# Two latent product pairs in one pass, and the next stage's gate rows and lambda made during the input projections

## The chip, the cores and the metric

One Trainium2 chip, one of its cores. The time is device microseconds of one launch. The kernel before took 2594.69 us (median of 3 runs, 2593.53 to 2594.82). The profiled execution took 2595.66 us, its span 2593.9 us, at a mean granted TensorE clock of 0.975 of full speed.

## The reference

One layer of an encoder with two attention branches over 2048 prompt tokens and 8 x 16 sample tokens that continue streams of 2048 cached positions. All of it is fp32.

```
h   = rms_norm(x, g_in)
qa, ka, va, z_a, qd, ckv_in, kpe_in, z_b, m_a, m_b = split(h @ w_in)
q1, q2, k1, k2 = rope of qa and ka, 4 heads            # differential branch
lam = exp(sum(lq1*lk1)) - exp(sum(lq2*lk2)) + lam_init
attn_a = (softmax(q1 k1) - lam * softmax(q2 k2)) v
q   = rms_norm(qd, g_qa) @ w_uq ; ckv = rms_norm(ckv_in, g_kva)   # latent branch, 4 heads
attn_b = softmax(q_nope . (ckv w_uk) + q_pe . kpe) (ckv w_uv)
y   = sigmoid(m_a) * (attn_a*silu(z_a)) @ w_oa + sigmoid(m_b) * (attn_b*silu(z_b)) @ w_ob
x   = rms_norm(x + y @ w_out)
```

Both softmaxes are causal by chunks of 64 tokens. New keys, values and latent rows are outputs too.

## The kernel before

Every fp32 product is made of three passes on TensorE: both factors are split into a high and a low part (`_split`, `_mm3`, L100 to L102 and L114/L115), and hi x hi, lo x hi, hi x lo are added in PSUM. For activations the split is a multiplication with the norm's factor on VectorE (scalar_tensor_tensor), a cast on ScalarE, and a subtraction on VectorE.

The program has these stages.

- *Input projections* (`_phase_a`). Three parts of the tokens (2 x 384, 2 x 384, 2 x 320). A part begins with its token rows x (L201 DMA, L202 scaling, L204 cast, L205 subtraction) and the product psv for the values (L246 to L248), which reads the first of them. Then come 11 pairs of column blocks. Each pair is made of seven products p1 to p7 in place of eight (`pair_products`, L327): p1 to p4 read the token tiles X[0], X[1]; p6, p7, p5 read sums of them, S[1], S[2], S[0]. Additions on VectorE (L335) put the seven together. The first pair is a latent one, eight rope and gate pairs follow, and the last two of a part are latent pairs again (l10 and l12 by name). Seven PSUM banks are shared by the products.
- *Latent stage* (`_phase_a2`). Six groups of 384 tokens (the last has 256): latent query products qn and qp, keys kn, values vb.
- *Attention* (`_phase_b`). Four heads of eight blocks; a block of the differential branch (sd, ed, od) runs paired with one of the latent branch (sm, em), so that each of the 32 pairs holds about the same work. At its start stands `_lam` (L1022), two small matmuls lam_ps and an exponential that give lam.
- *Sample tokens* and *output projections* at the end.

The gate columns (z_a, z_b, m_a, m_b) that the pairs don't make are made by `_gates` (L423): for each token group g, 16 units z_0 to z_15 of 24 matmuls each, all into one PSUM bank (tile z, freed by the tanh zt, L464). A unit loads 512 KB of weights (zs, two staging tiles) and splits them to zw (four tiles, two units' worth). Group 1 also writes its split weights to memory (wz, 1 MB a unit), and groups 2 and 5 read them back. A group's own rows are split first, into z_hi and z_lo (L433 to L443): one tile each, in the places that X[0] has in the input projections.

The order of instructions on each engine is set by a list scheduler that goes by priorities in program order. `_gates` is called after attention, so its matmuls come last by priority and fill places where TensorE would stand. Its loads, splits and tanh are raised (`ahead()`) to just behind the input projections.

```
_phase_a(c)
prio = tc.cur_priority
_phase_a2(c)
_phase_b(c)
for g in (0, 1, 2, 5):
    _gates(c, prio, g, None, g in (2, 5))
```

Of the kernel before, what the change touches and what calls it, by code (L numbers as in the profile page):

```python
# [46 lines left out]
def _consts(c, pool):  # L47
    nc = c.nc
    c.ident = pool.tile([P, P], F32, name="ident")
    make_identity(nc, c.ident)  # L50
    c.ones = pool.tile([P, P], F32, name="ones")
    nc.gpsimd.memset(c.ones, 1.0)
    c.mhalf = pool.tile([P, 64], F32, name="mhalf")
    nc.gpsimd.memset(c.mhalf, -0.5)
    c.vec = pool.tile([P, 20], F32, name="vec")
    nc.sync.dma_start(c.vec, c.i["vec"])
    c.g_in = c.vec[:, 0:8]
    c.g_qa = c.vec[:, 8:12]
# [70 lines left out]
def _phase_a(c):  # L129

    nc, tc = c.nc, c.tc
    with (
# [194 lines left out]
        def pair_products(p, u, nm):  # L327
# [13 lines left out]
            p4 = product(f"p4{nm}", a22, X[0], two)  # L341
            p6 = product(f"p6{nm}", s2, S[1], one)
            add(v, p6, m1)
            add(m1, p2, m1)
            p7 = product(f"p7{nm}", s3, S[2], one)
            add(u3, p7, v)
            p5 = product(f"p5{nm}", s1, S[0], one)
            add(v, p5, v)
            add(w, p5, u3)
            add(v, p3, v)  # L350
            add(u3, p4, u3)
            return (m1, v), (u3, w)

        def rope_pair(p, u, dst, pair, out, scale):
            t0, n = PARTS[p]
            res = pair_products(p, u, f"r{u}_{p}")
            for half in range(2):
# [21 lines left out]

        def latent_pair(p, u, out):  # L380
            t0, n = PARTS[p]
            res = pair_products(p, u, f"l{u}_{p}")
            for i, z in enumerate(res):
                for half in range(2):
                    nc.sync.dma_start(out[i][:, t0 + half * n : t0 + half * n + n], z[half])

        def gate_pair(p, u, out):
            t0, n = PARTS[p]
            res = pair_products(p, u, f"g{u}_{p}")
            for i in range(2):  # L390
# [5 lines left out]
        def pairs(p):  # L396
            rope = [lambda a=a: rope_pair(p, 2 * a, c.Qs, a, None, DIFF_SCALE) for a in range(2)]
            rope += [lambda a=a: rope_pair(p, 4 + 2 * a, c.Ks, a, c.o["kT"], 1.0) for a in range(2)]
            lat = [lambda a=a: latent_pair(p, 8 + 2 * a, [c.qdT[2 * a], c.qdT[2 * a + 1]]) for a in range(2)]
            lat.append(lambda: latent_pair(p, 12, [c.ckT[0], c.ckT[1]]))  # L400
# [7 lines left out]
        for p in range(len(PARTS)):  # L408
            raw = load_part(p)
            sums(p, raw)  # L410
            v_block(p)
            kpe_block(p)
            last_sum(p, raw)
            for i, f in enumerate(pairs(p)):
                f()
                if p + 1 < len(PARTS):
                    if i < 2 * PARTS[p + 1][1] // P:
                        squares(p + 1, i)
                    elif i == 6:
                        factors(p + 1)  # L420


def _gates(c, prio, g, after, ready):  # L423

# [5 lines left out]
    t0, n = GROUPS[g]  # L430
    with ahead():
        R = c.zh.tile([P, NG], F32, tag="R", name=f"Rz{g}")[:, :n]
        nc.sync.dma_start(R, c.Rh[:, t0 : t0 + n])  # L433
        hi = c.zh.tile([P, KT, NG], F32R, tag="hi0", name=f"z_hi{g}")[:, :, :n]
        lo = c.zh.tile([P, KT, NG], F32R, tag="lo0", name=f"z_lo{g}")[:, :, :n]
        for k2 in range(4):
            x = c.zs.tile([P, 2, NG], F32, tag="st", name=f"zx{g}_{k2}")[:, :, :n]
            nc.sync.dma_start(x, c.i["xT"][:, 2 * k2 : 2 * k2 + 2, t0 : t0 + n])
            for j in range(2):
                k = 2 * k2 + j  # L440
                nc.vector.scalar_tensor_tensor(x[:, j], x[:, j], c.g_in[:, k : k + 1], R, op0=ALU.mult, op1=ALU.mult)
                nc.scalar.copy(hi[:, k], x[:, j])
                nc.vector.tensor_tensor(lo[:, k], x[:, j], hi[:, k].bitcast(F32), op=ALU.subtract)  # L443
    for u in range(16):
# [215 lines left out]
def _lam(c, pool, psum):  # L660
# [7 lines left out]
    nc.scalar.activation(ex, ps[:, 0:2], AF.Exp)  # L668
    c.nlam = pool.tile([P, 1], F32, name="nlam")
    nc.vector.tensor_tensor(c.nlam, ex[:, 1:2], ex[:, 0:1], op=ALU.subtract)  # L670
# [335 lines left out]
def _phase_b(c):  # L1006
    nc, tc = c.nc, c.tc
    GQ = 256
    with (
# [11 lines left out]

        _lam(c, p1, lambda n: bank("o", n))  # L1022
        onesr = p1.tile([P, 32], F32R, name="onesr")
# [340 lines left out]
def build(tc, ins, outs, upto="z", dump=None):  # L1364
# [112 lines left out]
```

## Time and profile before

| | us |
|---|---|
| median of 3 runs | 2594.69 |
| profiled execution | 2595.66 |
| its span | 2593.9 |
| TensorE (PE) busy | 2418.1 (93%) |
| VectorE (DVE) busy | 1645.4 (63%) |
| ScalarE (ACT) busy | 1224.7 (47%) |
| gate matmuls L100 to L102, busy | 264.7, 257.9, 258.1 |

The stages, read from the timeline: input projections to about 621, latent stage to 862, attention from 888 to 1776, then sample tokens and output projections. Busy time counts a matmul from its start to its modelled end, and matmuls overlap: spacing of starts, not busy time, says how long a row of them takes.

### The profile page before, as it was taken

Reading aid. Unit: us, or ns where it says so; the run is one execution under the profiler, and the core shown is the slowest. Engines: PE = TensorE matmul, PEld = TensorE weight load, DVE = VectorE, ACT = ScalarE, POOL = GpSimd, SP = SyncE. Lnnn points to the kernel's source line nnn. Section 1 sums busy time; section 2 is a strip of 40 time slices with the busy share of each in tenths; the row PEclk is TensorE's granted clock in tenths of the full one; section 3 lists DMA queues with packets and bytes.
Section 4 is the critical chain, followed back from the end, with each engine's and each line's share of the span. In section 5 each row is a group of like instructions: output and inputs, shape, how many; then the busy total and the mean of one; then the engine's idle time right before and its main releaser. Section 6 shows DMA issues by size and latency. Waiting matters only on the chain. (4 is left out here: it accounts for less than half of the span.)

```text
span 2593.9 us, 44001 instructions
## 1 busy us (share of the span) xinstructions
PE 2418.1 (93%) x15426; PEld 2149.4 (83%) x15426; DVE 1645.4 (63%) x3668; ACT 1224.7 (47%) x3042; POOL 470.4 (18%) x730
## 2 busy tenths in 40 slices
PE   6998999997899699999999988998999997999998
PEld 5998999997888689899888977887676674988887
DVE  7897686886676477877776688894333223534334
ACT  5544544543444366766665566783334333311111
POOL 0000000000000032333343234443000002122211
PEclk9999999999899899999999999999999998999999
DMA  6977677686687986574666755316869594544332
GB/s 236 306 268 251 210 252 265 204 280 185 228 277 255 299 285 201 183 227 140 182 194 207 232 170 166 92 58 232 325 254 370 222 380 138 174 128 126 121 115 96
DMA packets 303997, 553.28 MB, mean 213 GB/s; under 512 B 29184, under 2 KB 230176, under 8 KB 288544
## 3 DMA queue, kind: packets, MB, share of 16 engines
q1 hardware_dynamic: 303776, 550.46, 64.0%
q8 instruction: 123, 2.02, 0.3%
q14 instruction: 98, 0.80, 0.1%
HBM read 397.16 MB, written 153.19 MB: 212 GB/s over the span
## 5 line engine op out<-in xcount | busy, mean ns | idle before, releaser
L100 PE MATMUL z<-z_hi,zw 128*128 128x384 f32 (+1 forms) x768 | 264.7, 345 | 47.1 <-ACT zt L464 28.2
L102 PE MATMUL z<-z_hi,zw 128*128 128x384 f32 (+1 forms) x768 | 257.9, 336 | 0.4 <-DVE zw L115 0.4
L101 PE MATMUL z<-z_lo,zw 128*128 128x384 f32 (+1 forms) x768 | 258.1, 336 | 0.1
L1079 ACT ACTIVATE ed<-sd,pmd 128x512 f32<-128x512 f32 (+3 forms) x320 | 201.1, 632 | 43.6 <-DVE pmd L1077 23.0
L1077 DVE TENSOR_REDUCE pmd<-sd 128x1 f32<-128x512 f32 (+3 forms) x320 | 189.4, 603 | 49.9 <-PE sd L1178 30.6
L1178 PE MATMUL sd<-k,q 128*128 128x512 f32 (+2 forms) x640 | 193.1, 391 | 13.3 <-ACT ed L1079 8.9
L100 PEld LDWEIGHTS z<-z_hi,zw 128*128 128x128 f32 x768 | 148.6, 193 | 68.6 <-ACT zt L464 36.1
L1118 POOL TENSOR_SCALAR ed<-ed,ad 128x512 f32<-128x512 f32 (+3 forms) x160 | 115.5, 737 | 317.5 <-DVE ad L1094 142.5
L101 PEld LDWEIGHTS z<-z_lo,zw 128*128 128x128 f32 x768 | 148.8, 194 | 7.3 <-issue 4.1
L102 PEld LDWEIGHTS z<-z_hi,zw 128*128 128x128 f32 x768 | 147.9, 193 | 6.5 <-issue 3.4
L109 POOL TENSOR_SCALAR ss<-ss 128x3 f32<-128x3 f32 (+3 forms) x15 | 3.2, 213 | 792.4 <-DVE ss L529 474.1
L115 DVE TENSOR_TENSOR zw<-zs,zw 128x512 fp32r<-128x512 f32 x128 | 84.4, 688 | 92.9 <-ACT zw L114 90.8
L100 PE MATMUL y<-o,wh_ab 128*128 128x384 f32 (+1 forms) x384 | 127.8, 333 | 13.7 <-DVE sm L1303 10.5
L1118 POOL TENSOR_SCALAR em<-em,am 128x512 f32<-128x512 f32 (+3 forms) x160 | 102.9, 660 | 185.5 <-DVE am L1094 115.5
L101 PE MATMUL y<-o,wh_ab 128*128 128x384 f32 (+1 forms) x384 | 126.6, 330 | 0.0
L102 PE MATMUL y<-o,wl_ab 128*128 128x384 f32 (+1 forms) x384 | 126.3, 329 | 0.0
L1178 PEld LDWEIGHTS sd<-k,q 128*128 128x128 f32 x640 | 105.4, 194 | 23.6 <-ACT ed L1079 15.5
L1079 ACT ACTIVATE em<-sm,pmm 128x512 f32<-128x512 f32 (+3 forms) x160 | 100.2, 629 | 47.0 <-DVE pmm L1077 34.2
L1303 DVE SCALAR_TENSOR_TENSOR sm<-sm,y 128x384 f32<-128x384 f32 (+1 forms) x96 | 50.4, 530 | 112.9 <-PE y L102 111.4
L1308 ACT ACTIVATE m<-sm 128x384 fp32r<-128x384 f32 (+1 forms) x48 | 24.3, 506 | 199.0 <-POOL sm L1306 199.0
L1077 DVE TENSOR_REDUCE pmm<-sm 128x1 f32<-128x512 f32 (+3 forms) x160 | 95.6, 603 | 35.3 <-PE sm L1225 27.4
L1135 ACT CAST pthd<-ptd 128x512 fp32r<-128x512 f32 (+3 forms) x160 | 82.6, 522 | 72.1 <-PE ptd L1132 69.6
(521 smaller groups left out, 7579.3 us busy)
## 6 DMA issues: line engine op xcount, KB each, us to landing
zs<-in_wu_dram SPq DMA_DIRECT2D x64, 512.0 KB
zw<-wz SPq DMA_DIRECT2D x64, 512.0 KB
ksd<-in_ckT_dram SPq DMA_DIRECT2D x32, 1024.0 KB
vsd<-in_cv_dram SPq DMA_DIRECT2D x32, 1024.0 KB
q<-Qs SPq DMA_DIRECT2D x128, 128.0 KB
wz<-zw SPq DMA_DIRECT2D x32, 512.0 KB
ksm<-in_cc_dram SPq DMA_DIRECT2D x16, 1024.0 KB
smT<-zt SPq DMA_DIRECT2D x80, 192.0 KB
```

The source lines that it names most:

```text
L100: nc.tensor.matmul(out, ah, bh, start=(j == 0), stop=False)
L101: nc.tensor.matmul(out, ah, bl, start=False, stop=False)
L102: last = nc.tensor.matmul(out, al, bh, start=False, stop=(j == n - 1))
L109: c.nc.gpsimd.tensor_scalar(ss, ss, scale, EPS, op0=ALU.mult, op1=ALU.add)
L115: nc.vector.tensor_tensor(lo, src, hi.bitcast(F32), op=ALU.subtract)
L1077: nc.vector.tensor_reduce(nm_, ps[:, :w], axis=AX.X, op=ALU.max, negate=True)
L1079: nc.scalar.activation(e[:, :w], ps[:, :w], AF.Exp, bias=nm_, accum_out=l[:, s, i : i + 1])
L1118: nc.gpsimd.tensor_scalar(p, p, a[:, 0, j : j + 1], 1.0, op0=ALU.mult, op1=ALU.mult)
L1135: nc.scalar.copy(hi, v)
L1178: nc.tensor.matmul(ps[:, :n], qs[s][:, j, qc], ks[s].tiles[i][:, :n], start=(j == 0), stop=(j == 1 and not last))
L1303: nc.vector.scalar_tensor_tensor(s, s, 1.0, ps, op0=ALU.add, op1=ALU.mult)
L1308: nc.scalar.mul(z[0], sm[0], 0.5)
```

## The change

Three edits.

1. *Latent pairs.* `pair_products` runs p1 to p4 and returns a function `finish` that runs p6, p7, p5 and the additions. `latent_pairs` calls the first half for both of a part's last pairs and then both second halves. Other pairs call both halves at once.
2. *Lambda.* `_lam` is called in the first part of the input projections, after `kpe_block`; its result tile c.nlam is allocated among the constants.
3. *Gate rows of group 0.* `_gate_rows` is the code that makes z_hi and z_lo, taken out of `_gates`. For group 0 it is called at the end of the input projections, with staging tiles of that stage ("cs") in place of zs, and `_gates` is handed the result.

```diff
             p4 = product(f"p4{nm}", a22, X[0], two)
-            p6 = product(f"p6{nm}", s2, S[1], one)
...
-            return (m1, v), (u3, w)
+
+            def finish():
+                p6 = product(f"p6{nm}", s2, S[1], one)
+                add(v, p6, m1)
+                add(m1, p2, m1)
+                p7 = product(f"p7{nm}", s3, S[2], one)
+                add(u3, p7, v)
+                p5 = product(f"p5{nm}", s1, S[0], one)
...
+                return (m1, v), (u3, w)
+
+            return finish
...
+        def latent_pairs(p, pairs):
+
             t0, n = PARTS[p]
-            res = pair_products(p, u, f"l{u}_{p}")
-            for i, z in enumerate(res):
...
+            todo = [(pair_products(p, u, f"l{u}_{p}"), out) for u, out in pairs]
+            for finish, out in todo:
+                for i, z in enumerate(finish()):
...
-            return [lat[0], *mixed, lat[1], lat[2]]
+            return [lambda: latent_pairs(p, lat[:1]), *mixed, lambda: latent_pairs(p, lat[1:])]
...
             kpe_block(p)
+            if p == 0:
+                _lam(c, pc, bank)
...
-def _gates(c, prio, g, after, ready):
+        c.rows = _gate_rows(c, 0, lambda name: pc.tile([P, 2, NG], F32, tag="cs", name=name, bufs=2))
...
+def _gates(c, prio, g, after, ready, rows=None):
...
-    with ahead():
-        R = c.zh.tile([P, NG], F32, tag="R", name=f"Rz{g}")[:, :n]
...
+    if rows is None:
+        with ahead():
+            rows = _gate_rows(c, g, lambda name: c.zs.tile([P, 2, NG], F32, tag="st", name=name))
+    hi, lo = rows
...
-        _lam(c, p1, lambda n: bank("o", n))
...
-                _gates(c, prio, g, None, g in (2, 5))
+                _gates(c, prio, g, None, g in (2, 5), c.rows if g == 0 else None)
```

The scheduler's order moves with it. On SyncE at the seam of parts 0 and 1, the load of x1_0_0 stood behind the outputs qdT, ckT<-m1l12 and the weight load ws_r0_1_1; now it stands right behind ckT<-m1l12, and ws_r0_1_1 is elsewhere. In the last part, TensorE now has p1 to p4 of l10, p1 to p4 of l12, then p6, p7, p5 of each, with the 24 matmuls of gate unit z0_0 in pieces between these; z0_0 to z0_8 stand ahead of the first latent query product, where z0_0 to z0_5 stood. The last unit of group 0 stands in the fifth token group, where it stood behind the sixth.

On ScalarE at the end of the input projections; z_hi0 are the rows of group 0, zw0_0_0 the high half of the weights of its unit 0, m1l12 the first product of the part's last pair, wh_uq the latent query weights. Before:

```order
L338 COPY m1l12_2_6477<-p1l12_2_6481 128x320
L442 CAST z_hi0_19636<-zx0_0_19638 128x384 x2
L442 CAST z_hi0_19636<-zx0_1_19646 128x384 x2
L442 CAST z_hi0_19636<-zx0_2_19654 128x384
L490 CAST onesr_6648<-ones_65 128x128
L442 CAST z_hi0_19636<-zx0_2_19654 128x384
L114 CAST wh_uq0_6608<-ws_uq0_6606 128x512
L442 CAST z_hi0_19636<-zx0_3_19662 128x384 x2
L114 CAST zw0_0_0_19670<-zs0_0_19672 128x512 x2
L114 CAST wh_uq1_6614<-ws_uq1_6612 128x512
L114 CAST zw0_0_1_19706<-zs0_1_19708 128x512 x2
```

And now:

```order
L339 COPY m1l12_2_6436<-p1l12_2_6440 128x320
L115 CAST zw0_0_0_19670<-zs0_0_19672 128x512 x2
L446 CAST z_hi0_6595<-zx0_0_6597 128x384 x2
L446 CAST z_hi0_6595<-zx0_1_6605 128x384 x2
L115 CAST zw0_0_1_19706<-zs0_1_19708 128x512 x2
L446 CAST z_hi0_6595<-zx0_2_6613 128x384 x2
L446 CAST z_hi0_6595<-zx0_3_6621 128x384 x2
L115 CAST zw0_0_2_19742<-zs0_2_19744 128x512 x2
L509 CAST onesr_6693<-ones_65 128x128
L483 ACTIVATE zt0_0_19703<-z0_0_19678 128x384
L115 CAST wh_uq0_6653<-ws_uq0_6651 128x512
```

The weights of units 0 to 2 and the rows now come ahead of the latent stage's weights.

On ScalarE between latent stage and attention; zt1_0 is the tanh of unit 0 of group 1, ed0_0 the first exponential of attention. Before:

```order
L464 ACTIVATE zt0_15_20243<-z0_15_20218 128x384
L442 CAST z_hi1_20248<-zx1_0_20250 128x384 x2
L442 CAST z_hi1_20248<-zx1_1_20258 128x384 x2
L588 CAST kz5_8325<-kp5_8315 64x256
L442 CAST z_hi1_20248<-zx1_2_20266 128x384 x2
L1024 CAST onesr_8364<-ones_65 128x32
L442 CAST z_hi1_20248<-zx1_3_20274 128x384 x2
L668 ACT_TABLE_LOAD
L668 ACTIVATE lam_ex_8359<-lam_ps_8357 128x2
L114 CAST zw0_1_0_20282<-zs1_0_20284 128x512 x2
L114 CAST zw0_1_1_20320<-zs1_1_20322 128x512 x2
L464 ACTIVATE zt1_0_20317<-z1_0_20292 128x384
```

And now:

```order
L483 ACTIVATE zt1_11_20735<-z1_11_20710 128x384
L115 CAST zw0_1_13_20776<-zs1_13_20778 128x512 x2
L483 ACTIVATE zt1_12_20773<-z1_12_20748 128x384
L1041 CAST onesr_8400<-ones_65 128x32
L115 CAST zw0_1_14_20814<-zs1_14_20816 128x512 x2
L483 ACTIVATE zt1_13_20811<-z1_13_20786 128x384
L115 CAST zw0_1_15_20852<-zs1_15_20854 128x512 x2
L483 ACTIVATE zt1_14_20849<-z1_14_20824 128x384
L483 ACTIVATE zt1_15_20887<-z1_15_20862 128x384
L1096 ACT_TABLE_LOAD
L1096 ACTIVATE ed0_0_0_0_0_8435,ld0_0_0_8425<-sd0_0_0_0_0_8430,pmd0_0_0_8424 128x128
```

Unit 0 of group 1 stood there alone; now all sixteen of its units, the last of them in one piece, stand ahead of the first exponential, and so does the table load that was lambda's.

On TensorE around the end of group 5's last unit, z5_15, in head 2; sd2_6 is a score product of differential block 6, sm2_5 one of latent block 5, ptm2_2 a transpose. Before:

```order
L100 MATMUL z5_15_21958<-z_hi5_21440,zw0_5_15_21954 128x256
L101 MATMUL z5_15_21958<-z_lo5_21441,zw0_5_15_21954 128x256
L1132 MATMUL ptm2_2_1_1_16079<-ident_60,em2_2_1_1_0_16062 128x128 x2
L1178 MATMUL sd2_6_0_2_1_16197<-k2_1_2_15405,q2_1_6_16138 128x512 x2
L102 MATMUL z5_15_21958<-z_hi5_21440,zw1_5_15_21955 128x256
L100 MATMUL z5_15_21958<-z_hi5_21440,zw0_5_15_21954 128x256
L101 MATMUL z5_15_21958<-z_lo5_21441,zw0_5_15_21954 128x256
L102 MATMUL z5_15_21958<-z_hi5_21440,zw1_5_15_21955 128x256
L1178 MATMUL sd2_6_0_3_0_16203<-k2_0_3_16141,q2_0_6_16135 128x256 x2
L1151 LDWEIGHTS maskq_73
```

And now:

```order
L101 MATMUL z5_15_21958<-z_hi5_21440,zw0_5_15_21954 128x256
L102 MATMUL z5_15_21958<-z_lo5_21441,zw0_5_15_21954 128x256
L1149 MATMUL ptm2_6_0_1_14571<-ident_60,em2_6_0_1_0_14535 128x128 x4
L103 MATMUL z5_15_21958<-z_hi5_21440,zw1_5_15_21955 128x256
L101 MATMUL z5_15_21958<-z_hi5_21440,zw0_5_15_21954 128x256
L102 MATMUL z5_15_21958<-z_lo5_21441,zw0_5_15_21954 128x256
L103 MATMUL z5_15_21958<-z_hi5_21440,zw1_5_15_21955 128x256
L101 MATMUL od2_1_14470<-pthd2_1_0_14405,v2_0_0_14047 128x256
L102 MATMUL od2_1_14470<-ptld2_1_0_14406,v2_0_0_14047 128x256
L103 MATMUL od2_1_14470<-pthd2_1_0_14405,v2_1_0_14049 128x256
```

The last gate unit before the sample tokens ended beside differential block 6 (latent block 1) and ends now beside differential block 2 (latent block 5): by my count of the pairs in the order, at pair 17.8 of 32 instead of 22.5.

## Rows read from the trace of the kernel before

**Rows 1.** What TensorE waits for: us in total, times, longest

```profile
PE z L100 <- ACT zt L464: 28.2, 21, 4.5
...
PE z L100 <- ACT zw L114: 18.9, 3, 10.9
PE psv L246 <- ACT xhi L204: 12.3, 3, 6.7
```

**Rows 2.** Busy time by stage, latent stage to head 2's end

```profile
core 0: us, PE busy (x) PEld busy (x) DVE busy (x) ACT busy (x) POOL busy (x), PEclk, DMA share, GB/s
678.80:862.60 183.80, 174.16 (x986) 167.94 (x985) 127.21 (x270) 80.91 (x166) 10.30 (x21) 0.97 0.81 260
862.60:881.90 19.30, 0.65 (x4) 0.54 (x3) 7.98 (x20) 7.42 (x17) 1.27 (x3) 0.56 0.81 244
881.90:887.80 5.90, 5.90 (x24) 5.67 (x25) 2.53 (x4) 1.57 (x3) 0.00 (x0) 0.70 1.08 334
887.80:1545.00 657.20, 640.42 (x4287) 582.00 (x4285) 484.54 (x1248) 419.22 (x1187) 224.39 (x364) 0.99 0.66 207
1545.00:1776.00 231.00, 209.25 (x1365) 176.34 (x1365) 198.74 (x520) 165.10 (x479) 97.55 (x148) 0.95 0.35 101
```

**Rows 3.** Same view, gate units (tile z) alone: PE, PEld, ACT, clock, DMA, GB/s

```profile
678.80:862.60 183.80, 49.64 (x240) 44.97 (x240) 4.89 (x10) 0.97 0.81 260
887.80:1545.00 657.20, 216.53 (x1130) 180.14 (x1128) 21.94 (x48) 0.99 0.66 207
```

**Rows 4.** Timeline (start, duration, engine, line, operation, idle before): seams of the parts

```profile
240.40 0.91 SPq L201 DMA_DIRECT2D x<-in_xT_dram  x2
...
245.34 1.13 DVE L202 SCALAR_TENSOR_TENSOR x<-x,vec,R 128x384 f32<-128x384 f32 x2
...
246.54 0.80 PE L246 MATMUL psv<-wv,xhi 128*128 128x512 f32 x1 [6.66 <-ACT xhi L204]
...
451.33 0.50 PE L246 MATMUL psv<-wv,xhi 128*128 128x512 f32 x1 [2.81 <-ACT xhi L204]
```

**Rows 5.** TensorE's timeline, input projections to latent stage

```profile
631.77 0.69 PE L100 MATMUL z<-z_hi,zw 128*128 128x384 f32 x1 [10.89 <-ACT zw L114]
...
649.38 0.44 PE L100 MATMUL z<-z_hi,zw 128*128 128x384 f32 x1 [4.19 <-ACT zt L464]
...
657.04 0.44 PE L100 MATMUL z<-z_hi,zw 128*128 128x384 f32 x1 [0.96 <-ACT zt L464]
...
665.97 0.69 PE L100 MATMUL z<-z_hi,zw 128*128 128x384 f32 x1 [4.49 <-ACT zt L464]
...
678.80 0.42 PE L100 MATMUL qn<-qh,wh_uq 128*128 128x384 f32 x1
```

**Rows 6.** TensorE's timeline, one gate unit after a wait

```profile
827.04 0.45 PE L100 MATMUL z<-z_hi,zw 128*128 128x384 f32 x1 [4.43 <-ACT zt L464]
...
831.15 0.33 PE L102 MATMUL z<-z_hi,zw 128*128 128x384 f32 x1
831.32 0.33 PE L100 MATMUL z<-z_hi,zw 128*128 128x384 f32 x1
```

**Rows 7.** Timeline, latent stage to attention

```profile
862.28 0.34 PE L102 MATMUL z<-z_hi,zw 128*128 128x384 f32 x1
...
873.70 1.28 ACT L668 ACT_TABLE_LOAD   x1
...
873.83 0.58 PE L666 MATMUL lam_ps<-lam_pr,ones 128*128 128x2 f32 x2 [11.21 <-DVE lam_pr L664]
...
874.57 0.53 SPq L453 DMA_DIRECT2D zs<-in_wu_dram  x1
...
881.19 1.14 ACT L114 CAST zw<-zs 128x512 fp32r<-128x512 f32 x2 [6.02 <-DMA zs<-in_wu_dram]
...
881.86 0.69 PE L100 MATMUL z<-z_hi,zw 128*128 128x384 f32 x1 [7.45 <-ACT zw L114]
...
887.82 0.40 PE L1178 MATMUL sd<-k,q 128*128 128x256 f32 x2
```

More of the change, by code (lines that the diff above doesn't have):

```diff
@@ L61, in _consts @@
     nc.vector.tensor_scalar(c.gsub, c.vec[:, 14:15], 1.0 - LAM_INIT, None, op0=ALU.mult)
+    c.nlam = pool.tile([P, 1], F32, name="nlam")
     c.maskq = pool.tile([P, P], BF16, name="maskq")
@@ L341, in pair_products @@
             p4 = product(f"p4{nm}", a22, X[0], two)
-            p6 = product(f"p6{nm}", s2, S[1], one)
[L343 to L351, printed above, removed]
-            return (m1, v), (u3, w)
+            def finish():
[5 more added lines that the diff above has]
+                p5 = product(f"p5{nm}", s1, S[0], one)
+                add(v, p5, v)
+                add(w, p5, u3)
+                add(v, p3, v)
+                add(u3, p4, u3)
+                return (m1, v), (u3, w)
+            return finish
         def rope_pair(p, u, dst, pair, out, scale):
             t0, n = PARTS[p]
-            res = pair_products(p, u, f"r{u}_{p}")
+            res = pair_products(p, u, f"r{u}_{p}")()
             for half in range(2):
@@ L378, in rope_pair @@
                         nc.sync.dma_start(dst[pair, hl, a, :, cols], z)
-        def latent_pair(p, u, out):
+        def latent_pairs(p, pairs):
             t0, n = PARTS[p]
-            res = pair_products(p, u, f"l{u}_{p}")
-            for i, z in enumerate(res):
-                for half in range(2):
-                    nc.sync.dma_start(out[i][:, t0 + half * n : t0 + half * n + n], z[half])
+            todo = [(pair_products(p, u, f"l{u}_{p}"), out) for u, out in pairs]
+            for finish, out in todo:
+                for i, z in enumerate(finish()):
+                    for half in range(2):
+                        nc.sync.dma_start(out[i][:, t0 + half * n : t0 + half * n + n], z[half])
         def gate_pair(p, u, out):
             t0, n = PARTS[p]
-            res = pair_products(p, u, f"g{u}_{p}")
+            res = pair_products(p, u, f"g{u}_{p}")()
             for i in range(2):
@@ L398, in pairs @@
             rope += [lambda a=a: rope_pair(p, 4 + 2 * a, c.Ks, a, c.o["kT"], 1.0) for a in range(2)]
-            lat = [lambda a=a: latent_pair(p, 8 + 2 * a, [c.qdT[2 * a], c.qdT[2 * a + 1]]) for a in range(2)]
-            lat.append(lambda: latent_pair(p, 12, [c.ckT[0], c.ckT[1]]))
+            lat = [(8 + 2 * a, (c.qdT[2 * a], c.qdT[2 * a + 1])) for a in range(2)] + [(12, (c.ckT[0], c.ckT[1]))]
             gate = [lambda a=a: gate_pair(p, 14 + 2 * a, [c.gzT[2 * a], c.gzT[2 * a + 1]]) for a in range(4)]
             mixed = [f for z in zip(rope, gate) for f in z]
-            return [lat[0], *mixed, lat[1], lat[2]]
+            return [lambda: latent_pairs(p, lat[:1]), *mixed, lambda: latent_pairs(p, lat[1:])]
         for t in range(2 * PARTS[0][1] // P):
@@ L420, in _phase_a, with _gate_rows @@
                         factors(p + 1)
-def _gates(c, prio, g, after, ready):
+        c.rows = _gate_rows(c, 0, lambda name: pc.tile([P, 2, NG], F32, tag="cs", name=name, bufs=2))
+def _gate_rows(c, g, get):
+    nc = c.nc
+    t0, n = GROUPS[g]
+    R = c.zh.tile([P, NG], F32, tag="R", name=f"Rz{g}")[:, :n]
+    nc.sync.dma_start(R, c.Rh[:, t0 : t0 + n])
+    hi = c.zh.tile([P, KT, NG], F32R, tag="hi0", name=f"z_hi{g}")[:, :, :n]
+    lo = c.zh.tile([P, KT, NG], F32R, tag="lo0", name=f"z_lo{g}")[:, :, :n]
+    for k2 in range(4):
+        x = get(f"zx{g}_{k2}")[:, :, :n]
+        nc.sync.dma_start(x, c.i["xT"][:, 2 * k2 : 2 * k2 + 2, t0 : t0 + n])
+        for j in range(2):
+            k = 2 * k2 + j
+            nc.vector.scalar_tensor_tensor(x[:, j], x[:, j], c.g_in[:, k : k + 1], R, op0=ALU.mult, op1=ALU.mult)
+            nc.scalar.copy(hi[:, k], x[:, j])
+            nc.vector.tensor_tensor(lo[:, k], x[:, j], hi[:, k].bitcast(F32), op=ALU.subtract)
+    return hi, lo
+def _gates(c, prio, g, after, ready, rows=None):
     nc, tc = c.nc, c.tc
@@ L430, in _gates @@
     t0, n = GROUPS[g]
-    with ahead():
-        R = c.zh.tile([P, NG], F32, tag="R", name=f"Rz{g}")[:, :n]
[L433 to L443, printed above, removed]
+    if rows is None:
+        with ahead():
+            rows = _gate_rows(c, g, lambda name: c.zs.tile([P, 2, NG], F32, tag="st", name=name))
+    hi, lo = rows
     for u in range(16):
```

1 line of the change is left out of this document (removed).

## The prediction

> **What bounds the kernel now.** I read the list of waits first, then a table of windows by stage, then the timeline of the seams between stages. In the table [rows 2] TensorE is busy 174.16 of the 183.8 us of the latent stage and 640.42 of the 657.2 us of attention up to head 2, while VectorE has 127.21 and 484.54 there: within a stage TensorE is the bound. What isn't TensorE's work lies at the seams. The waits [rows 1] name them: 28.2 us for the one PSUM bank of the gate units, 18.9 us in three waits for a unit's split weights, 12.3 us in three waits for a part's first token rows. The seam of latent stage and attention is one hole, 862.60 to 881.90 with 0.65 us of TensorE work [rows 2].
>
> The gate units are what fills holes. A unit is 24 matmuls of 384 columns; at the full clock they start 0.17 us apart (831.15, 831.32 in [rows 6]; over the rest of that unit 0.174), so a unit is 24 x 0.174 = 4.18 us. In attention up to head 2, 1130 gate matmuls are woven in [rows 3]: units 1 to 15 of group 1, 16 of group 2, 16 of group 5 (two thirds as wide). After 1545 there are none, and TensorE is busy only 209.25 of 231.0 us [rows 2].
>
> The sum is made against the profiled run, 2595.66 us (span 2593.9, 1.8 around it); the median of the runs is 1 us below it, and I take that off at the end.
>
> **Seams of the parts: -3.0.** At the first, the wait is 6.66 us, at the second 2.81 [rows 4]. The chain there is x's DMA at 240.40, its scaling on VectorE at 245.34, the cast, psv. Both orders show what changes: that DMA stood behind a weight load (ws_r0_1_1) and the output ckT<-wl12; the weight load is now elsewhere, and the products that read the x tiles come earlier, the sum products last. I estimate the DMA some 2.9 us earlier. Against it, with p1 to p4 of two pairs in seven banks, p7 of the first pair needs a bank that only an addition behind p6 frees: I estimate 1.3 us a part. I take -2.0 and -1.0. The ends are -9.5 (both waits gone) and +3.9 (the bank wait in all three parts, nothing gained).
>
> **Lambda: 0.** Its wait of 11.21 us at 873.83 looks like a prize, but behind it TensorE's next instruction, the gate unit at 881.86, waits a further 7.45 us for the cast of zw at 881.19, whose load was issued at 874.57 [rows 7]. The matmul stands in the shadow of that chain. Alone, its removal gives 0 there. In the input projections it is two small matmuls; ends 0 and +6.7 (the longest wait of that kind, [rows 1]) if TensorE stops for VectorE's lam_pr. The table load of 1.28 us at 873.70 [rows 7] also stands in that shadow and moves to the first exponential, on the path to attention: it is in the ramp below. The Trainium skill, "ScalarE: Activation LUTs", What ACT_TABLE_LOAD costs, puts a switch at about 2.66 us with its drain; the trace has the load at 1.28, and by the page the sum would be 1.4 us worse.
>
> **Group 0's rows in the input projections: -11.5, -6.1.** Before, the first unit starts at 631.77 after 10.89 us for its weights, and the unit at 649.38 after 4.19 more; six units are done when the first latent query product comes at 678.80 [rows 5]. In the new order unit 0 stands between the last sum products, and nine units stand ahead of that product: three more by about the same time, 3 x 4.18 = 12.5, less 1 us that the latent stage's own first load comes later. The wait of 4.43 at 827.04 goes, since group 0 is over by then, and with it the slow matmuls behind the wait: 24 at 0.174 would have brought the engine from 827.04 to 831.2, and the fifteenth stood at 831.15 [rows 6], so 14 x 0.174 = 2.4 us of work took 4.1, 1.7 more. 4.43 + 1.7 = 6.1. The ends: 0 and -15 for the first (TensorE may simply stop at units 3 to 8, for the same loads), 0 and -6.1 for the second.
>
> **The hole before attention: -19.2.** Group 1's rows can only be made when group 0's last unit has freed the two row tiles, and then a chain runs: last matmul 862.28, new rows, weights' load 874.57, cast 881.19, unit at 881.86 [rows 7]. From 862.6 to 881.86 that is 19.2 us. In the new order group 0's last unit stands in the middle of the fifth of six token groups. The latent stage without its ten gate units [rows 3] and the 6.1 us is 183.8 - 41.8 - 6.1 = 136 us for 5.67 groups, 24 each; behind that place lie half a group and the short last one, 12 + 16 = 28 us. So group 0 ends about 816, and the same chain, 19 us, runs beside 28 us of work that needs nothing of it. The end on the other side is -8, if that work comes too late.
>
> **What takes their place: +11.2 and +3.** The order shows all 16 units of group 1 ahead of attention's first product, units 5 to 15 in one piece. One PSUM bank passes from unit to unit, so each waits for its tanh: the wait at 657.04 is 0.96 [rows 5], so I take 5.2 us a unit instead of 4.18, for eleven units +11.2. Such a unit reads 0.52 MB of weights, writes 1.05 MB of split weights and 0.2 MB of result: 1.77 MB in 5.2 us is 340 GB/s, near the 334 of the stretch around 885 [rows 2], so the transfers allow no more either. Ends: 0, and +37 at the pace of the seam at 631.77, (665.97 - 631.77)/4 = 8.55 us a unit [rows 5]. Behind the last unit attention has nothing else to run: its first keys and queries are loaded after the units' weights, and the table load stands before the first exponential. In the trace the first product follows a unit at once, 887.82 [rows 7]; I take +3, ends 0 and +8.
>
> **Attention without group 1: +13.2.** The 15 units removed from it cost nothing by being moved (their 62.6 us are spent earlier), but fillers now end earlier: by the order at pair 17.8 of 32 instead of 22.5. An unfilled pair takes 231.0/9.5 = 24.3 us [rows 2]; a filled one, its gate matmuls (744 x 0.174 + 384 x 0.116 = 174.0; two thirds of the columns taken as two thirds of the time) taken out, (657.2 - 174.0)/22.5 = 21.5. So 4.7 pairs x 2.8 = 13.2. Ends 0 and +18.
>
> **Sum:** -3.0 - 11.5 - 6.1 - 19.2 + 11.2 + 3 + 13.2 = -12.4; 2595.66 - 12.4 - 1 = 2582.3, said as 2582.
>
> **Rivals.** (a) *The block of gate units is not paced by TensorE; slower.* Place: units 5 to 15 of group 1. The tanh that frees the bank shares ScalarE's queue with the casts of later units, and a cast that waits for its load holds it up; that is the seam at 631.77, where units came 8.55 us apart. Price: eleven units at 7 to 8.55 us cost 20 to 37 us beyond my term, so 2602 to 2620. It decides from 5.2 + 12.4/11 = 6.3 us a unit. For it: 1.77 MB a unit, and the granted clock fell to 0.70 of full around the unit at 881.86, which after a wait of 7.45 us took 5.96 us [rows 2, 7]. Against it: after 0.96 us of wait the unit at 657.04 ended at 665.97 - 4.49 = 661.48, so 4.44 us [rows 5], nearly the full clock, and ScalarE then has little else. Of (a)'s 0.24, 0.06 are for the clock alone: every one of the eleven units at 5.96 instead of 4.18 is +19.6, so 2602. The Trainium skill, "TensorE: Matmul & The Clock Gate", A second HAM failure mode: psum-queue depth-cycling, speaks for that and so against this change: an engine that pauses at each PSUM group may swing between its two clocks. The unit at 657.04 disagrees.
>
> (b) *Fillers aren't missed; faster.* If the late pairs wait on what a filler wouldn't cover, +13.2 is 0: 2569. For it: 21.75 us of idle in 9.5 pairs, 2.3 each, is less than the 2.8 I used. Against it: with fillers TensorE was idle 16.8 us in 22.5 pairs [rows 2].
>
> (c) *The same loads are waited for elsewhere; no change.* Rows made early don't bring weights earlier than two staging tiles allow, and their scaling and splitting share VectorE with the last pairs' additions: units 0 to 8 wait as units 0 to 5 did, the first term is 0, and the time 2582 + 11.5 = 2594. For it: the seam's DMA traffic; against it, three units' loads stand before the end of the input projections in the order.
>
> **Chances.** My sum 0.44, (a) 0.24, (b) 0.14, (c) 0.18. Two measurements of this kernel differ by up to 0.2%, about 5 us: faster by more 0.58, within it 0.18, slower 0.24. The forecast's own range is 2574 to 2589. Eight times in ten: 2562 (below (b)) to 2608 (half of (a)).
>
> **What would show it.** After: no wait for xhi above 5 us; nine units before the first latent query product, at about 678; the last unit of group 0 near 816; no hole of 19 us; sixteen units of group 1 about 5.2 us apart in a block; attention's first product near 925 (887.8 - 39.8 for the seams + 15 x 4.18 for the units + 14.2) (before 887.82); the last gate matmul of group 5 between 1430 and 1460; attention's remaining stretch some 50 us shorter than before, counted from its first product. The prediction is wrong in its main step if the block's units are over 6.3 us apart, or the clock there is well below 0.9.

## The result, and the profile after

The changed kernel took 2607.72 us (median of 4 runs, 2605.38 to 2612.46), beside 2594.76 us of the kernel before: ratio 1.0059, interval 1.0045 to 1.0073. Measured again with more runs it was 1.0077 (1.0059 to 1.0095). The prediction was 2582 us and faster; it is slower, by 13 us and then 20. Executions of one kernel lie up to 0.6% apart here (before: 2581.09 to 2596.74 in one set of 27), so a difference of 3 us in one stage of one profile is not read.

The stages of the two profiles, from TensorE's timeline (us from the start; gate units done in brackets), with two kernels of the experiments (sd is attention's first product):

| | before | changed | no lambda move (e13) | changed, tile kept (e10) |
|---|---|---|---|---|
| psv of part 2 | 451.3 | 457.0 | 454.9 | 457.5 |
| first latent query product | 678.8 (6) | 692.6 (9) | 681.3 (8) | 693.0 (9) |
| first attention product | 887.8 (17) | 940.6 (32) | 920.5 (28) | 936.9 (32) |
| attention's last differential product (od) | 1775.6 | 1782.8 | 1767.0 | 1784.3 |
| first differential sample score (ssd) | 1794.8 | 1796.5 | 1786.2 | 1802.0 |
| last differential sample score | 2116.9 | 2128.5 | 2104.7 | 2125.6 |
| last output product | 2583.8 | 2597.2 | 2566.8 | 2588.1 |

What TensorE waited for after, the lines that answer to [rows 1] (us in total, times, longest):

```profile
PE z L101 <- ACT zt L483: 32.2, 29, 3.8
...
PE psv L247 <- ACT xhi L205: 12.9, 3, 6.5
...
PE z L101 <- ACT zw L115: 1.1, 1, 1.1
```

The waits for split weights, 18.9 us in three before, are down to one of 1.1, and lambda's 11.2 us are gone. The wait for the gate units' bank grew from 28.2 to 32.2 us, and that for a part's first rows is what it was. The seams of the parts, answering to [rows 4] (start, duration, engine, line, operation, idle before), first two rows of before:

```profile
237.16 0.43 SPq L385 DMA_DIRECT2D ckT<-m1l  x1
...
446.55 0.45 SPq L201 DMA_DIRECT2D x<-in_xT_dram  x1
```

They are the output ckT<-m1l ahead of the x load of [rows 4], and the first x load of part 2. Now:

```profile
239.87 1.97 SPq L202 DMA_DIRECT2D x<-in_xT_dram  x2
...
244.22 0.38 SPq L392 DMA_DIRECT2D ckT<-m1l  x1
244.65 0.94 SPq L202 DMA_DIRECT2D x<-in_xT_dram  x2
...
250.71 0.79 PE L247 MATMUL psv<-wv,xhi 128*128 128x512 f32 x1 [6.54 <-ACT xhi L205]
...
451.78 0.42 SPq L202 DMA_DIRECT2D x<-in_xT_dram  x1
...
457.00 0.79 PE L247 MATMUL psv<-wv,xhi 128*128 128x512 f32 x1 [3.60 <-ACT xhi L205]
```

The x load of [rows 4], at 240.40 before, is issued at 244.65. It stands right behind the output ckT<-m1l, as the order said, but that output is itself issued 7.1 us later. The first x load of part 2 comes 5.2 us later. psv waits 6.54 us again, and 3.60 at the next part. The start of the latent stage, answering to [rows 5]:

```profile
633.52 0.45 PE L101 MATMUL z<-z_hi,zw 128*128 128x384 f32 x1 [0.63 <-ACT zt L483]
...
642.14 0.62 ACT L115 CAST wh_uq<-ws_uq 128x512 fp32r<-128x512 f32 x1 [2.74 <-DMA ws_uq<-in_wuq_dram]
644.39 1.48 ACT L532 ACTIVATE sq<-qd 128x1536 f32<-128x1536 f32 x1 [1.63 <-DMA qd<-qdT]
645.78 1.12 ACT L115 CAST zw<-zs 128x512 fp32r<-128x512 f32 x2
646.81 0.48 ACT L483 ACTIVATE zt<-z 128x384 f32<-128x384 f32 x1
...
647.34 0.69 PE L101 MATMUL z<-z_hi,zw 128*128 128x384 f32 x1 [3.43 <-ACT zt L483]
...
687.01 0.44 PE L101 MATMUL z<-z_hi,zw 128*128 128x384 f32 x1 [1.58 <-ACT zt L483]
```

From 633.52 to 687.01 seven units pass, 7.6 us each. The tanh at 646.81, which frees the bank, stands on ScalarE behind a cast of wh_uq and a square of qd, both idle before for loads of the latent stage: 2.74 and 1.63 us. The end of the block, answering to [rows 7]:

```profile
888.66 0.44 PE L101 MATMUL z<-z_hi,zw 128*128 128x384 f32 x1 [0.58 <-ACT zt L483]
...
893.68 0.44 PE L101 MATMUL z<-z_hi,zw 128*128 128x384 f32 x1 [0.58 <-ACT zt L483]
...
924.69 1.32 SPq L472 DMA_DIRECT2D zs<-in_wu_dram  x1
...
929.67 0.44 PE L101 MATMUL z<-z_hi,zw 128*128 128x384 f32 x1 [0.58 <-ACT zt L483]
...
932.40 0.54 SPq L1047 DMA_DIRECT2D k<-Ks  x1
...
940.60 0.51 PE L1195 MATMUL sd<-k,q 128*128 128x256 f32 x2 [1.48 <-DMA k<-Ks]
```

From 888.66 to 929.67 there are eight steps, 5.1 us a unit; most are 5.01, with a wait of 0.58 for the tanh. Attention's first keys are issued at 932.40, behind the last weights of a gate unit, and its first product waits for them. The stages by windows, answering to [rows 2] (span, then busy us and instructions of PE, PEld, DVE, ACT, POOL; clock, DMA share, GB/s):

```profile
692.50:940.60 248.10, 229.75 (x1293) 219.08 (x1292) 148.58 (x309) 105.98 (x216) 12.12 (x24) 0.99 0.90 304
888.70:940.60 51.90, 44.59 (x241) 41.07 (x241) 14.63 (x27) 18.56 (x39) 0.87 (x3) 1.00 1.03 369
940.60:980.60 40.00, 30.01 (x118) 20.96 (x119) 21.02 (x53) 17.54 (x51) 5.98 (x10) 0.74 1.01 327
980.60:1440.50 459.90, 453.75 (x3140) 413.93 (x3139) 355.97 (x917) 301.85 (x862) 169.67 (x283) 1.00 0.62 188
1440.50:1782.80 342.30, 310.82 (x2036) 260.55 (x2035) 289.48 (x770) 244.81 (x712) 142.09 (x220) 0.98 0.37 106
```

The second line is the block's end: 240 gate matmuls and one more, at a clock of 1.00 and a DMA share of 1.03. The third is the finding: in attention's first 40 us TensorE has 118 matmuls at a granted clock of 0.74. The same 40 us before, and then the gate matmuls alone in these two stretches, before and after:

```profile
887.80:927.80 40.00, 37.29 (x206) 32.21 (x205) 21.10 (x51) 20.91 (x58) 7.81 (x13) 1.00 1.01 358
```

```profile
887.80:927.80 40.00, 18.86 (x98) 16.55 (x96) 2.48 (x5) 1.00 1.01 358
...
940.60:980.60 40.00, 4.34 (x18) 2.96 (x18) 0.00 (x0) 0.74 1.01 327
```

206 matmuls at 1.00 before, but 98 of them are gate matmuls, against 18 now: attention's own are 108 and 100. So attention's own work took these 40 us with the gate units and without them, and what is missing now is room that was filled before, 80 gate matmuls or 13.9 us at 0.174. The last window, 342.3 us for 14.2 pairs without gate units, is 24.1 us a pair, as the prediction took it.

### The profile page after: what moved, and what is told of

The parts are those of the page before. It is cut to its first block, busy times and chain, and to the rows that moved or that the text cites. A ratio compares the mean times of both kernels' runs of the same rounds, so it can differ in the third digit from the quotient of the medians.

```text
span 2607.3 us, 44029 instructions
## 1 busy us (share of the span) xinstructions
PE 2437.0 (93%) x15426; PEld 2151.8 (83%) x15426; DVE 1646.1 (63%) x3668; ACT 1227.0 (47%) x3042; POOL 465.9 (18%) x730
## 5 line engine op out<-in xcount | busy, mean ns | idle before, releaser
L101 PE MATMUL z<-z_hi,zw 128*128 128x384 f32 (+1 forms) x768 | 264.1, 344 | 34.8 <-ACT zt L483 32.2
L1135 POOL TENSOR_SCALAR ed<-ed,ad 128x512 f32<-128x512 f32 (+3 forms) x160 | 109.6, 700 | 273.7 <-DVE ad L1111 116.6
L1325 ACT ACTIVATE m<-sm 128x384 fp32r<-128x384 f32 (+1 forms) x48 | 24.3, 507 | 199.4 <-POOL sm L1323 199.2
L1153 DVE TENSOR_TENSOR ptlm<-ptm,pthm 128x512 fp32r<-128x512 f32 (+3 forms) x160 | 96.1, 602 | 33.3 <-ACT pthm L1152 32.4
```

What stands on the lines that cost most here:

```text
L101: nc.tensor.matmul(out, ah, bh, start=(j == 0), stop=False)
L1135: nc.gpsimd.tensor_scalar(p, p, a[:, 0, j : j + 1], 1.0, op0=ALU.mult, op1=ALU.mult)
L1153: nc.vector.tensor_tensor(ptl[ch][:, :n, i * P : (i + 1) * P], v, hi.bitcast(F32), op=ALU.subtract)
```

## The experiments

Theory 1 looks to the early parts, theory 2 to the block of gate units ahead of attention; the others came as these fell. Ratios are to the kernel before, measured beside.

**e1 to e4: the three parts apart.** Each is the kernel before with one edit of the three, or the changed kernel without lambda's move.

> Kernel before with lambda alone moved into the input projections. Theory 1 (the early parts pay: lambda's small steps shift the order of VectorE's queue in part 0, where a normal addition then stands behind a load): psv of part 1 about 3 us later than before (246.5 to 249.5), p3r's wait for m1g near 3.0 instead of 1.8, time about 2597 to 2598. Theory 2 (the loss is the block of gate units ahead of attention and what it takes from attention): this kernel keeps group 1's units in attention, so no change, 2594 to 2596.

> Kernel before with the two latent pairs run together alone; in the order this alone puts group 1's block ahead of attention. Theory 1: the second pair's results hold token tiles longer, x of the next part is loaded 3 to 4 us later, psv of part 1 comes 1 us later than before and not earlier; time about 2597 to 2600. Theory 2: the same time as the whole change, 2605 to 2609, since the block is there.

> Kernel before with group 0's gate rows made at the end of the input projections alone. Theory 1: seams of the parts as before (psv 246.5 and 451.3), first latent query product near 678 to 682 with six units ahead; time 2592 to 2597. Theory 2: the block is ahead of attention here too, so 2602 to 2609.

> The whole change without lambda's move. Theory 1: lambda's 3 us come back, psv of part 1 near 247.5, time 2604 to 2605. Theory 2: within 2 us of the whole change, 2606 to 2609.

Measured, against expectations given in us on a kernel before of 2594.7: lambda alone 1.0025 (1.0011 to 1.0038), pairs alone 1.0062 (1.0045 to 1.0079), rows alone 1.0005 (0.9992 to 1.0019), pairs and rows 0.9962 (0.9948 to 0.9975). The parts don't add: without lambda's move the change is a gain of 0.4%. Lambda's psv of part 1 came at 244.8 (246.5 to 249.5 expected), so theory 1's reason for it fell; pairs alone came out near theory 2, rows alone near theory 1, and pairs with rows where neither had it. Rows alone had the first latent query product at 665.7 in its profile, 13 us earlier, and its ratio shows that gain lost behind it.

**e5, e6: both kernels again, beside each other.**

> The kernel before, unchanged, for a profile on the chip of these runs. Every theory: its time as the kernel before shown beside it, and psv of part 1 at 245 to 247, first attention product near 884 to 888.

> The whole change, unchanged, measured beside the kernels without one of its parts. Theory 2 (the block): 1.004 to 1.008 of before, as first measured. Theory 3 (the times of the first comparison hung on the chip it ran on): near 0.996, as the change without lambda's move gave.

e5 took 2589.87 us, its first attention product at 886.9; e6 1.0077 (1.0059 to 1.0095). Theory 3 fell: lambda's move costs some 1.1% inside the whole change (1.0077 against e4's 0.9962).

**e7, e8: group 1's matmuls held back.**

```diff
-                _gates(c, prio, g, None, ...)
+                _gates(c, prio, g, c.first.ins if g == 1 else None, ...)   # c.first: attention's first product
```

> The whole change, with the matmuls of group 1's sixteen units ordered behind attention's first product, so that they are fillers of attention again. Theory 2 (the loss is the block: 16 units 5.0 us apart where 4.18 would do, and attention thinned by 14 units too many): first attention product near 860 to 872, last unit of group 5 later again, near 1520 to 1540, and the time 25 to 30 us below the whole change, 0.993 to 0.996 of before. Theory 1 (the early seams lost it, 5.7 us at part 2 and 8 more at the latent stage): the block's place is worth 5 us at most, 1.003 to 1.006 of before.

> Group 0's rows made early alone, with group 1 held behind attention's first product. Theory 2: the 13 us that this edit had won at the first latent query product and the hole of 19 us before attention both reach the end: 0.987 to 0.992 of before. Theory 1: 0.998 to 1.001, as without the hold.

1.0064 (1.0046 to 1.0082) and 0.9988 (0.9977 to 0.9999). Theory 2 fell as I had sized it; the times are near theory 1's, though not for its reason. In e7 attention's first product came at 890.1, 56 us earlier than in e6, and attention with its sixteen units took 888.2 us instead of 845.2, so a unit costs 5.1 in the block and 2.7 as a filler. But ahead of the first product TensorE waits for attention's keys, and has nothing to fill that wait with:

```profile
890.06 0.55 PE L1195 MATMUL sd<-k,q 128*128 128x256 f32 x1 [18.07 <-DMA k<-Ks]
```

e8 waits 9.99 us there in the same way, so the hold is no clean test of theory 2. And e7's sample scores took 341.7 us, where e8's took 319.2.

**e9, e10, e11: lambda's tile.** Of the kernels so far, each one with lambda moved, and none other, had the sample tokens' work in another order on TensorE. The order changes already if only the tile's allocation moves (e9 has the changed kernel's), so it isn't lambda's arithmetic. e9 moves that one line; e10 gives attention's pool a copy:

```diff
+        nlam = p1.tile([P, 1], F32, name="nlam_b")
+        nc.vector.tensor_copy(nlam, c.nlam)
+        c.nlam = nlam
         onesr = p1.tile([P, 32], F32R, name="onesr")
```

> The kernel before, with one line moved: the tile of lambda's result is allocated among the constants instead of in attention's pool; lambda is still made at attention's start, and all engines' orders are as before up to the sample tokens. Theory 4 (the tile in attention's pool was what the first sample loads had to wait for; without it they start earlier, the scheduler weaves gate units into the latent score chain, and a later load comes late): sample scores begin about 12 us behind attention's last product instead of 18, last about 332 us instead of 322, time 1.002 to 1.005 of before. Theory 5 (lambda's steps in part 0 cost the time, not its tile): 1.000, within 0.001.

> The whole change, with one tile and one copy added: attention's pool holds a copy of lambda, as it held lambda before. TensorE's order is that of the whole change up to the sample tokens, and there that of the kernel before. Theory 4: sample scores last 318 to 323 us instead of 332 to 334, time 5 to 12 us below the whole change, 1.002 to 1.005 of before. Theory 5: no change from the whole change, 1.006 to 1.008.

> As the last, and group 1's matmuls held behind attention's first product as well. Theory 4: the hold alone gave 1.0064 and its sample scores lasted 342 us, so 20 us less there: 0.998 to 1.000 of before. Theory 5: 1.005 to 1.007.

e9: 0.9995 (0.9984 to 1.0005), a miss: its sample scores began 13.7 us behind attention and took 330.1, which together is 3 us more than in e5, and nothing in the time. e10: 1.0028 (1.0016 to 1.0040), 13 us below the whole change by the ratios, within the ratio expected. e11: 1.0009 (0.9996 to 1.0022), 14 us below e7, short of the 20 expected and a little above the range. In the changed kernel gate matmuls stand inside the chain of the first latent sample scores:

```profile
1796.46 1.06 PE L841 MATMUL ssd<-ksd,sp 128*32 128x512 f32 x8
...
1835.37 1.07 PE L926 MATMUL ssm<-kTsm,sp 128*64 128x512 f32 x2
1836.37 0.66 PE L914 MATMUL ktsm<-ident,ksm 128*128 128x128 f32 x4
1836.78 0.42 PE L103 MATMUL z<-z_hi,zw 128*128 128x384 f32 x1
...
1862.76 0.33 SPq L838 DMA_DIRECT2D ksd<-in_ckT_dram  x1
```

In e10 one whole unit stands behind the chain's first scores, at 1828.88, and the next gate matmul comes at 1857.26, when the chain is through:

```profile
1801.95 1.06 PE L841 MATMUL ssd<-ksd,sp 128*32 128x512 f32 x8
...
1853.32 0.33 SPq L838 DMA_DIRECT2D ksd<-in_ckT_dram  x1
```

The load of the keys (ksd) that needs a freed tile comes 66.3 us behind the first sample score in the one, 51.4 in the other, and the stage's loads follow it. Why the allocation lets the scheduler choose that order was not shown.

**e12: the hold without lambda's move.**

> The change without lambda's move, with group 1's matmuls held behind attention's first product. Theory 4 says nothing on the hold: the block's place was worth 0.001 to 0.002 so far, so 0.994 to 0.997 of before. If attention thinned by fourteen units were the cost (theory 2), 0.986 to 0.990.

1.0000 (0.9988 to 1.0011): worse than with four units only behind attention's first product (e4), so neither theory's number. Here too TensorE waits for the keys with nothing to fill the wait:

```profile
886.01 0.58 PE L1194 MATMUL sd<-k,q 128*128 128x256 f32 x1 [9.91 <-DMA k<-Ks]
```

Of the places tried, the sixteen units did best neither all ahead nor all behind.

**e13, e14: is the gain real, and what pairing does at the seams.** e14 is the kernel of e13 with pairing in the last part alone:

```diff
+            tail = [lat[1:]] if p == 2 else [lat[1:2], lat[2:]]
```

> The change without lambda's move, again, as the one version below the kernel before. Theory 6 (its gain is real: four gate units stand behind attention's first product there and are taken up by its first stretch): 0.994 to 0.998 of before. Theory 7 (0.38% is what placement or the day gives; the block's place is neutral, as the hold said): 0.999 to 1.001.

> As the last, but the two latent pairs run together in the last part alone; parts 0 and 1 run them one after the other as before. Theory 8 (pairing holds the token tiles and the outputs longer, so that x of the next part is loaded later): psv of part 1 at 244 to 247 instead of 250, of part 2 at 449 to 452 instead of 457, time 3 to 5 us below the last, 0.992 to 0.996. Otherwise: psv of part 1 stays near 250 and the time within 2 us of the last.

e13: 0.9960 (0.9945 to 0.9975), so 0.4% is real. Its psv of part 2:

```profile
454.91 0.80 PE L246 MATMUL psv<-wv,xhi 128*128 128x512 f32 x1 [3.60 <-ACT xhi L204]
```

And that of e14:

```profile
451.32 0.50 PE L246 MATMUL psv<-wv,xhi 128*128 128x512 f32 x1 [2.55 <-ACT xhi L204]
```

3.6 us earlier, as theory 8 has it. The first x load of part 2 is at 446.79 there, beside 446.55 before and 451.78 in the changed kernel. psv of part 1 came at 246.5, only 1.0 us before e13's. But e14 took 0.9964 (0.9950 to 0.9978), the same time. The seam's loss exists and was given back before attention (first product at 920.5 and 921.4).

**e15: the latent stage's start without the units' loads.** Group 0's units 1 to 15 split the weights that unit 0 loaded.

```diff
-                st = c.zs.tile(...); nc.sync.dma_start(st, c.i["wu"][22 + u])
+                if g or u == 0:
+                    st = c.zs.tile(...); nc.sync.dma_start(st, c.i["wu"][22 + u])
```

> The whole change with lambda's copy kept, and group 0's units 1 to 15 without a load of weights of their own: each splits the tile that unit 0 loaded (so these gates are not the reference's). Theory 9 (at the latent stage's start the units wait for the same loads as before, rival c): units there 5.0 to 5.9 us apart instead of 7.6. Theory 10 (ScalarE and VectorE, shared with the latent stage's own splits, set the pace): 7 us or more still.

The first and the sixth of these units in e15, and below the first, the sixth and the eighth in e10:

```profile
631.75 0.45 PE L101 MATMUL z<-z_hi,zw 128*128 128x384 f32 x1 [0.63 <-ACT zt L484]
...
666.68 0.44 PE L101 MATMUL z<-z_hi,zw 128*128 128x384 f32 x1 [1.91 <-ACT zt L484]
```

```profile
632.46 0.45 PE L101 MATMUL z<-z_hi,zw 128*128 128x384 f32 x1 [0.63 <-ACT zt L483]
...
672.80 0.69 PE L101 MATMUL z<-z_hi,zw 128*128 128x384 f32 x1 [3.94 <-ACT zt L483]
...
687.51 0.45 PE L101 MATMUL z<-z_hi,zw 128*128 128x384 f32 x1 [1.48 <-ACT zt L483]
```

(666.68 - 631.75)/5 = 7.0 us a unit, against (672.80 - 632.46)/5 = 8.1 over the same units (7.9 up to the eighth). Theory 10, more than 9: of 3.0 us over the 5.1 of the block, the units' own loads make 1.1. For the rest the trace points to ScalarE's queue, where the tanh stands behind casts that wait for the latent stage's own loads, as in the rows at 642.14 to 646.81 above; no run took those loads away. The whole took 2563.88 us in one run, but the order changed elsewhere too (16 units ahead of attention), so that says nothing on the loads alone.

**e16: lambda alone, its tile kept.** Besides the copy of lambda, attention's pool holds two more small tiles here, in place of the two others that `_lam` had there.

> Lambda alone moved, with attention's pool holding a copy. Theory 4 (what lambda alone cost, 1.0025, was its tile's place): 0.998 to 1.001, sample scores 320 to 326 us. Theory 5 (its steps in part 0 cost it): 1.002 to 1.004 still.

0.9997 (0.9984 to 1.0010) against 1.0025: lambda's steps in part 0 cost nothing that shows. But e9, with the tile moved and the steps left at attention's start, cost nothing either, so the 0.25% of lambda alone came with the two together and is no price of the tile by itself. e16's order of the sample tokens is neither that of before nor that of e9.

**e17, e18: units put where the faster kernel has them.**

```diff
+                _gates(c, prio, g, (lambda u: c.first.ins if u >= 12 else None) if g == 1 else None, ...)
```

> The whole change with lambda's copy kept, and group 1's last four units alone held behind attention's first product, as the kernel without lambda's move has them. Theory 11 (with all units ahead, attention's first 40 us have nothing to fill its waits for loads: 118 matmuls there at a clock of 0.74, against 206 at 1.00 before): first product about 917, the 40 us behind it near 200 matmuls at 1.00, the end of attention 10 to 16 us earlier, 0.996 to 0.999 of before. Theory 12 (four units cost the same 5 us wherever they stand): no change, 1.002 to 1.004.

> As the last, and group 0's ninth unit held behind the first latent query product, where the kernel without lambda's move has it. Theory 11, and the units at the latent stage's start, 7.9 us apart, delaying it: first latent query product near 683 instead of 693, 2 to 5 us below the last, 0.995 to 0.998 of before: the gain of the change without lambda's move, lambda's move and all. Otherwise, if lambda's steps themselves cost it: within 1 us of the last or above it.

1.0035 (1.0022 to 1.0048) and 1.0052 (1.0035 to 1.0069): both missed. e18's first latent query product came at 692.4 with eight units ahead, where e17's came at 693.0 with nine, so holding the ninth gained nothing. For the rest, e17 shows why:

```profile
914.62 0.44 PE L101 MATMUL z<-z_hi,zw 128*128 128x384 f32 x1 [0.58 <-ACT zt L484]
...
924.54 1.12 SPq L472 DMA_DIRECT2D zs<-in_wu_dram  x1
...
930.92 1.01 SPq L1051 DMA_DIRECT2D k<-Ks  x2
...
938.83 0.77 PE L1199 MATMUL sd<-k,q 128*128 128x256 f32 x2 [19.78 <-DMA k<-Ks]
```

The four units are out of the way, and TensorE waits 19.78 us for attention's keys, whose load is issued at 930.92, behind the last units' weights at 924.54; in e10 it was issued at 929.39. Holding four units' matmuls did not bring the load forward. Behind the first product the units do what theory 11 says of them, 209 matmuls in 40 us:

```profile
938.83:978.83 40.00, 40.00 (x209) 35.57 (x210) 23.86 (x62) 21.36 (x62) 10.30 (x17) 0.93 1.00 329
```

So the load would have to come earlier too. In e13:

```profile
911.57 1.01 SPq L1046 DMA_DIRECT2D k<-Ks  x2
...
920.48 0.40 PE L1194 MATMUL sd<-k,q 128*128 128x256 f32 x2
```

There the keys are issued at 911.57, while three units' weights are still to come, and the first 40 us of attention are full:

```profile
920.50:960.50 40.00, 36.95 (x201) 31.62 (x200) 20.03 (x49) 20.74 (x57) 8.77 (x16) 1.00 1.00 337
```

Not all of the 19 us between the two loads is the queue's order: the latent stage's last product comes at 873.3 in e13 and at 883.5 in e17.

What fills those 40 us is the number of group 1's units that are left, not the time of the keys. With none left (changed, e2, e6, e10) they hold 111 to 118 matmuls at a clock of 0.70 to 0.74. With one left (e3) they hold 133 at 0.87, though its keys were issued at 916.87, as early as e4's. With four left (e4, e13, e14, e17, e18) they hold 194 to 209 at 0.93 to 1.00. Attention as a whole shows the same. From its first to its last differential product, with each unit moved out of it counted at 4.18 us, it took 16 to 22 us more than before with none or one left, and 2 to 6 us more with four left. In e17 and e18 that gain was there too, but the wait for the keys (19.78 and 16.79 us) stood against it. A kernel that moves the loads alone was not tried.

## Why the prediction was wrong

By its own steps, in the first pair of profiles, with the work of a moved unit counted at 4.18 us:

- *Seams of the parts: -3.0.* Measured +5.7 at psv of part 2, beyond the end of +3.9 that I gave. This step failed by its direction: I moved the x loads ahead by the row that stood in front of them, and did not ask when the output that they now stand behind would be ready. With both pairs finished late, ckT<-m1l came 7.1 us later and the loads 4.3 and 5.2 us later instead of 2.9 earlier. e14 shows that pairing makes psv of part 2 later, by 3.6 us; in all profiles psv of part 2 is at 454.3 to 460.4 with parts 0 and 1 paired and at 448.3 to 453.0 without. Whether the token tiles are held longer too was not shown apart. It didn't matter for the time in e14.
- *Lambda: 0.* Its wait was in the shadow, as said: alone it gained nothing, and in e13, with lambda still at attention's start, 1.33 us of the wait are left. But the step failed where I took its move for its instructions alone: in the whole change it costs some 1.1%. With its tile gone from attention's pool the sample stage was ordered otherwise; putting a copy back took 13 of 20 us away (e10), and 14 us with the hold (e11). That it is no fixed price shows in e9, where the same order cost nothing. The rest of the 1.1% lies mostly in attention, as is worked out below.
- *Group 0's rows: -11.5.* Measured 692.6 - 678.8 - 5.7 - 3 x 4.18 = -4.5. I had counted three more units in about the same time; they came 7.6 us apart, the tanh behind casts that wait for loads. That is rival (c)'s place and rival (a)'s mechanism, and I had given each to the other.
- *-6.1, -19.2, +11.2 and +3, from there to attention's first product: -11.1.* Measured (940.6 - 692.6) - (887.8 - 678.8) - 12 x 4.18 = -11.2. These steps held. The block ran at 5.1 us a unit (I took 5.2), the clock was 1.00 through its last 51.9 us, and the wait ahead of attention's first product was 1.48 us (I took 3). So rival (a) fell there: waits of 0.58 us between units cost their length and no clock. The Trainium skill, "TensorE: Matmul & The Clock Gate", A second HAM failure mode: psum-queue depth-cycling, tells of an engine that idles briefly between groups of matmuls and swings between its two clocks; this block's 1.00 doesn't show that.
- *Attention without group 1: +13.2.* Measured (1782.8 - 940.6) - (1775.6 - 887.8) + 15 x 4.18 = +17.1. The size is near, the make-up isn't, so that nearness is in part luck. By my own count of pairs, the thin pairs cost 24.1 x 14.2 - (21.5 x 4.7 + 24.3 x 9.5) = +10. The room for 80 gate matmuls in the first 40 us, which units of group 1 had filled at no cost to attention, went unused: +14. Behind it the filled pairs had less idle time, 6.2 us from 980.6 to 1440.5, against 14.1 from 927.8 to 1545 before: -8. The second of these I had put at nothing: I counted the fifteen units as 62.6 us wherever they stand, and called the order of attention's loads a ramp of 3 us.
- *Nothing behind attention.* Measured (2597.2 - 1782.8) - (2583.8 - 1775.6) = +6.2. With the copy of lambda back in the pool (e10) the same stretch took 803.8 us instead of 814.4.

The sum of these is 5.7 - 4.5 - 11.2 + 17.1 + 6.2 = 13.3, the spans' difference (2607.3 - 2593.9 = 13.4). The forecast had -12.4. The largest single failures are the early seams (8.7 us) and the latent stage's start (7.0); by the experiments, what decides the sign is lambda's move, since without it the same edits give 0.996. The time fell where rival (a) had put its own, 2602 to 2620, but that is luck: the block it spoke of ran as I had forecast.

What lambda's move costs besides its tile is the step from e13 to e10, 0.996 to 1.003. Between their profiles, with four units more ahead of attention in e10, the first attention product differs by 936.9 - 920.5 - 4 x 4.18 = -0.3, attention by (1784.3 - 936.9) - (1767.0 - 920.5) + 4 x 4.18 = +17.6, and all behind it by +4.0. So by the profiles most of it is the room in attention that four units would have filled, and none of it the latent stage's start. No experiment gave it back, because e17 and e18 moved the units and not the loads; why the scheduler puts all sixteen units ahead when lambda is moved stays open.

I had also taken 0.2% as the difference between two measurements, where executions of one kernel lay up to 0.6% apart. Of the signs I named, the last unit of group 0 (816.5 to 822), the last gate matmul of group 5 (1440.6) and the block's pace and clock came; the waits for xhi (6.54 us), the first latent query product (692.6) and attention's first product (940.6) did not.

## What to carry to other kernels

An edit under a list scheduler is not only its instructions: a tile that leaves a pool can reorder a stage far behind it, so compare the order of every stage, and try each part alone and all but each part. Before fillers are moved ahead of a stage, count how many matmuls they had in that stage's first stretch and what its own work does there without them: here 80 gate matmuls had cost attention nothing. Ask too where the fillers' loads stand in the DMA-issuing queue against that stage's first loads; holding four units' matmuls back (e17) did not bring those loads forward. Price a waiting seam by what stands ahead of the evicting instruction on its engine, and not by the producer's own loads alone. When an edit moves a load up in a queue, ask when the row it now stands behind is ready.

## What was not expected of the hardware

Waits of 0.58 us after units of 4.43 us (one of 1.09 us) left the clock at 1.00 over 240 matmuls, while attention's first 40 us, with 30 us of busy TensorE in many pieces, had 0.74. Before, attention's first 40 us took in 98 gate matmuls and still 108 of its own, where it had 100 of its own without them. By the scheduler and not by the hardware, a tile of four bytes a partition, put back into attention's pool, changed the time by some 0.5% in two kernels (e10, e11), and moving it changed nothing in a third (e9).
